# A two-layer trunk (RG-LRU, then forgetting attention) on one core: other output blocks kept on the chip, short rows' logits spread in three runs, the last squares in a tile of their own

## The chip, the core and the metric

The kernel runs on one core of a Trainium2 chip. The core has five engines, each with its own stream of instructions that it works through in order: TensorE (PE, matrix products; PEld is its loading of weights), VectorE (DVE), ScalarE (ACT), GpSimd (POOL) and SyncE (SP). SP computes nothing here: it issues transfers, as POOL does too. Transfers are carried out by 16 DMA engines. The metric is the time of one execution on the device, in microseconds (us), as the median of several runs.

## The reference

One sequence of 1024 tokens and width 1024 goes through two layers and a last norm. Everything is fp32.

```
for i in range(DEPTH):                      # DEPTH = 2
    h = rms_norm(x, norm_g[i])
    if i % 2 == 0:  x = x + lru_mixer(h, ...)   # layer 0
    else:           x = x + fox_mixer(h, ...)   # layer 1
return rms_norm(x, final_g)
```

Layer 0 (`lru_mixer`): `u = h @ w_in` (1024 to 3072) gives a branch and a gate of 1536 channels each; the branch passes a causal convolution over 4 tokens; two block-diagonal products give the gates `r` and `i`; a linear recurrence over the tokens runs with `a = exp(-8 r softplus(-a_param))`; its result times `silu(gate)` is projected back by `w_out`.

Layer 1 (`fox_mixer`), the one that the change touches most:

```
q, k, v, gate, f = split(h @ w_in)                 # 16 heads of 64
cum    = cumsum(log_sigmoid(f + b_f))              # per head
logits = q k^T / 8 + cum[query] - cum[key], causal
o      = softmax(logits) v
y      = (o * silu(gate)) @ w_out
```

## The kernel before

**Number format.** Each fp32 operand is split into a high and a low part (`hh`/`hl`, `wh`/`wl`, `yhh`/`yhl` and so on), and a product is three TensorE passes: high by high, high by low, low by high. A weight block comes by a transfer into a buffer `wf`, ScalarE casts it to `wh` (L90), and VectorE subtracts to get `wl` (L101). All matrix products are issued by the helper at L60, all plain loads of this kind by `fetch` (L56 and L57) on SP.

**Stages of a run.** Times are those of the profiled execution. Layer 0 fills the time from 0 to about 460 us. The rest is layer 1, head by head (`hd` 0 to 15). For a head there are two runs. The first multiplies the weights of queries 0 to 511 of this head with its values (`weigh(hd, 0)`, PSUM tile `O`) and makes the logits of queries 512 to 1023 (`maxima(hd, 1)`, PSUM tiles `S`, two of them). The second run does `weigh(hd, 1)` and `maxima(hd + 1, 0)`, the logits of the next head's short rows: row block i has 128(i+1) keys, so blocks 0 to 3 have 128 to 512.

**One row block in `maxima`.** TensorE makes `S`; VectorE adds the mask and finds the row maximum (L786); ScalarE takes the exponential into `p` (L791); VectorE scales the row sum and inverts it (L797, L798); ScalarE and VectorE write the high and the low half of the weights `pp` (L92, L800); SP issues a transposing transfer `pT<-pp` (L802). `weigh` reads the four blocks of `pT`. ScalarE and VectorE then collect `O` (L829, L830), and `gated` multiplies with the gate (L839) and stores the head pair's result to memory (`y1d<-yo`).

**What sets the order.** The two runs are written as strings, at L29 (`ORDER`, and `LAST` for heads 12 and on). In `run`, a digit takes one step of `weigh` (0) or `maxima` (1), and a dot takes one step of *filling* work: six matrix passes of the projections for later heads, in heads 12 to 15 of the output projection. Each step is tied behind the TensorE instruction before it. Apart from these ties a scheduler with a cost model of its own places the instructions of every engine when the program is built, so an edit in one place can change the order in others.

**Values.** After heads 3, 7 and 11 stand the values of the next four heads (`values(g)`, PSUM tiles `vps`, eight token blocks of eight products each, three passes a product). Their weights `in_wv` come in four chunks of 256 KB, two products each.

**Output.** From about 943 us on, the filling work is the output projection of the first six head pairs (`partial`, PSUM tiles `ops` of the two buffers with tag `g`): for each of 8 blocks of output channels `db` and 2 halves of tokens `c`, twelve groups of passes, plus the stored residual `x1d` (L924). Most blocks go by a round trip: POOL loads the residual (L921) into one of two buffers `xp`, VectorE adds, POOL stores it back (L926), and SP loads it once more at the end. For half 0, four blocks are *kept*: their sum stays in a tile that has become free. Blocks 3 and 2 share the tile of the gate (`sg`, named `x3`), blocks 4 to 7 the tile of one set of keys (`T0`, named `x4`). The last stage (`turned`, `finish`) adds the last two head pairs, transposes and normalizes.

**Start.** Layer 0 begins with the sum of squares of x. Half h's first seven squares are added on VectorE into one tile (`m2`); the eighth is left in a working tile (`ti`, L266) and joined by a matrix product with ones (`rsrow`). Square root and inversion (3.35 us on VectorE) give the row factor `rs`.

**Middle.** Between the layers, the sum of squares of the new x works alike (`squares`, `inv_rms`): the last block's square is a second operand of the `sscol` products for each half.

Of the kernel before, what the change touches and what calls it, by code (L numbers as in the profile page):

```python
# [16 lines left out]
AF = mybir.ActivationFunctionType  # L17
# [3 lines left out]
SEQ = 1024  # L21
HALF = 512
KT = 8
# [2 lines left out]
HD = 64  # L26
EPS = 1e-6
GROUP = 2
ORDER = "1.1..1.1..00", "1.1.1.1...0000"  # L29
LAST = "1..1..1..1..0.0", "1..1.1..1..0..0.0.0"  # L30
NEG = -1e30
PSUM = bass.MemoryType.PSUM
# [8 lines left out]
def trunk(ctx: ExitStack, tc: tile.TileContext, xt, w0, wg, wo0, pc, gn, gf, w1, wv, wf, bf, wo1, out):  # L41
    nc = tc.nc
# [16 lines left out]
    def matmul(*args, **kw):  # L59
        pe[0] = nc.tensor.matmul(*args, **kw)  # L60
        return pe[0]
# [8 lines left out]
    onesf = const.tile([P, P], F32, name="onesf")  # L70
    nc.vector.memset(onesf, 1.0)
    epst = const.tile([P, 1], F32, name="epst")
# [49 lines left out]
    def weights(src, parts=wpool, lo_eng=nc.gpsimd):  # L122

        for k in range(0, src.shape[1], 4):
            n = min(4, src.shape[1] - k)
            yield from split_weights([(src[:, k : k + n], slice(0, P))], (n, P), nc.scalar, lo_eng, parts)
# [13 lines left out]
    def drain(gen):  # L140
        for _ in gen:
            pass
# [42 lines left out]
    halves = (slice(0, HALF), slice(HALF, SEQ))  # L185

    late = ctx.enter_context(ExitStack())
    with ExitStack() as l0:
# [12 lines left out]
        def long(tag, dtype=F32, bufs=1):  # L201
            return tmp.tile([P, SEQ], dtype, tag=tag, name=tag, bufs=bufs)
# [29 lines left out]
        xs = [[xpool.tile([P, HALF], F32, name=f"x{h}{k}") for k in range(KT)] for h in range(2)]  # L232
        first = ([], [])
        early = [weights(w0[0], lo_eng=nc.vector), weights(w0[NB], lo_eng=nc.gpsimd)]
        k = 0
# [12 lines left out]
        sums = [[], []]  # L248
# [8 lines left out]

        acc = long("m2")
        sq = [z[:, cs] for z in (long("th"), long("ti")) for cs in halves]

        def square_x(h):
            to = acc[:, halves[h]]
            sums[h].append(to)
            for k in range(KT):
                z = sq[k % 4] if k else to
                nc.scalar.activation(z, xs[h][k], AF.Square)  # L266
                if k == KT - 1:
                    sums[h].append(z)
                elif k:
                    nc.vector.tensor_tensor(to, to, z, ALU.add)  # L270
                yield
# [4 lines left out]
        def norm_row(h):  # L276

            row = ps.tile([P, HALF], F32, tag="O", name="rsrow")
            for i, sq_ in enumerate(sums[h]):
                matmul(row, onesf, sq_, start=i == 0, stop=i == len(sums[h]) - 1)  # L280
            r_ = rs[:, halves[h]]
            nc.scalar.activation(r_, row, AF.Sqrt, bias=epst, scale=1.0 / SEQ)
            return nc.vector.reciprocal(r_, r_)

        for _ in zip(split_x(0), square_x(0)):
            pass
# [2 lines left out]
        state = {}  # L289
# [119 lines left out]
        for n in range(NB):  # L409
            wu = first[0] if n == 0 else list(weights(w0[n]))  # L410
            if n == 1:
                ups = both = [ps.tile([P, HALF], F32, tag="g", name="ups") for h in range(2)]
            else:
                ups = two_banks("ups")
                both = [ups.rearrange("p a b -> p (a b)")]
                ups = [ups[:, h] for h in range(2)]
            product(ups[0], 0, wu)
            if n == 0:
                gps = held[0] = two_banks("gps")
                product(gps[:, 0], 0, first[1])  # L420
                for _ in zip(split_x(1), square_x(1)):
                    pass
                done = norm_row(0)
            else:
                gates(n - 1)
                if n > 1:
                    with tc.issue_after(state[n - 1]["last"].ins):
                        outputs(n - 2)
            product(ups[1], 1, wu)
            if n == 0:  # L430
                product(gps[:, 1], 1, first[1])
                norm_row(1)
                with tc.issue_after(done.ins):
                    softplus()
            conv(n, both)
            if n % 2 and n > 1:
                fill = itertools.chain(fill, project_out((n - 3) // 2))
            take(fill, 4)
            if n > 3:
                with tc.issue_after(state[n - 1]["last"].ins):  # L440
                    take(vsquares, 4)
            if n > 1:
                wn = list(weights(w0[NB + n - 1]))
                gps = held[n - 1] = two_banks("gps")
                for h in range(2):
                    product(gps[:, h], h, wn)
            if n:
                drain(silu(state[n - 1], held.pop(n - 1)))

                with tc.issue_after(state[n]["tap"].ins):  # L450
                    recur(n - 1)
            take(fill, 4)
# [45 lines left out]
        for h, cs in enumerate(halves):  # L498
            y = [tuple(z[:, cs] for z in p) for p in ys[-2:]]
            hT[h] = [pair() for k in range(KT)]  # L500
            parts = split_x(h, 1)
            sums = []
            for d0 in range(0, KT, 4):
                pts = []
                for db in range(d0, d0 + 4):
                    if db % 2 == 0:
                        two = ps.tile([P, 2, HALF], F32, tag="S", name="ops")
                    pts.append(two[:, db % 2])
                    mm3(pts[-1], wl[db][0], y[0], True, False)
                for db, o in enumerate(pts, d0):  # L510
                    mm3(o, wl[db][1], y[1], False, True)
                    x = xs[h][db]
                    nc.vector.tensor_tensor(x, x, o, ALU.add)  # L513
                    nc.sync.dma_start(x1d[h, :, db], x)
                    next(parts)
                    squares(
                        sums,
                        x,
                        lambda: nrm.tile([P, HALF], F32, tag="sq" if db else "ss", name="sq", bufs=2),
                        wait=db == KT - 1,  # L520
                    )
            rms_row(sums, rs1[h], rms1[h])
            if h == 0:
                value_bounds()
            nc.vector.tensor_tensor(
                rv[:, :, 4 * h : 4 * h + 4],
                rms1[h].unsqueeze(1).to_broadcast([P, 4, 4]),
                scale_v.unsqueeze(2).to_broadcast([P, 4, 4]),
                ALU.mult,
            )  # L530
# [7 lines left out]
    with ExitStack() as l1:  # L538
# [190 lines left out]
        first = values(0)  # L729
# [170 lines left out]
        homes = {}  # L900

        def home(db):

            if db == 3:
                two = at.tile([P, 2, HALF], F32, tag="sg", name="x3")
                homes[3], homes[2] = two[:, 0], two[:, 1]
            elif db == 5:
                four = tu.tile([P, 4, HALF], F32, tag="T0", name="x4")
                homes.update((4 + i, four[:, i]) for i in range(4))
            return homes[db]  # L910

        def partial(todo):

            for db, c in todo:
                split_out(db)
                if c if db < 2 else not c:
                    split_out(db + 1)

                kept = c == 0 and db in (3, 5, 6, 7)
                x = home(db) if kept else rpool.tile([P, HALF], F32, tag="R", name="xp")  # L920
                nc.gpsimd.dma_start(x, x1d[c, :, db])  # L921
                pt = ps.tile([P, HALF], F32, tag="g", name="ops1")
                yield from gemm_steps(pt, zip(wo[db], [y1[c][pair] for pair in range(6)]))
                nc.vector.tensor_tensor(x, x, pt, ALU.add)  # L924
                if not kept:
                    nc.gpsimd.dma_start(x1d[c, :, db], x)  # L926
# [5 lines left out]
        def residual(c, q):  # L932

            cs = slice(q * 256, (q + 1) * 256)
            if c == q == 0:
                two = tu.tile([P, 2, HALF], F32, tag="U0", name="x0")
                homes[0], homes[1] = two[:, 0], two[:, 1]
                for d in (0, 1, 2, 4):
                    fetch(homes[d], x1d[c, :, d])
            if c == 0:  # L940
                return [homes[d][:, cs] for d in range(KT)]
            xs = [wpool.tile([P, 2, 256], F32, tag=("wl", "wh")[q], name="x1") for d in range(4)]
            for d, x in enumerate(xs):
                fetch(x, x1d[c, :, 2 * d : 2 * d + 2, cs])
            return [x[:, i] for x in xs for i in range(2)]
# [107 lines left out]
        for hd in range(HEADS):  # L1053
# [21 lines left out]
                    )  # L1075
            elif pair < 6:
                fill = chain(g_units(pair + 1), kq_units(pair + 2, ((1, (0,)),)))
            first, second = LAST if hd > 11 else ORDER
            if hd == HEADS - 1:
                first = "1..1.0.1.0.1..."  # L1080
            side = chain(pieces(hd + 1, 0, 0), pieces(hd + 1, 0, 1)) if hd else iter(())
# [105 lines left out]
```

## Time and profile before

| | us |
|---|---|
| median of 3 runs | 1081.56 (1079.12 to 1083.71) |
| profiled execution | 1079.6 |
| its span in the profile | 1077.8 |
| outside the span | 1.8 |
| TensorE busy | 1048.0 (97%) |
| VectorE busy | 782.1 (73%) |
| ScalarE busy | 621.6 (58%) |

The page of the profile lists busy time by engine and by group of instructions. A line of a group or of the timeline ends with the idle time of the engine just ahead of the instruction, and what ended it: `[5.52 <-DVE sums L797]` says that the engine stood still for 5.52 us and that VectorE's instruction of that line was the last one that it waited for. The table of windows gives busy time by stretch, the clock granted to TensorE as a share of full speed, the share of time in which the DMA engines were at work, and the rate of the transfers. Transfers on SP and POOL stand in the timeline with the time that their issue takes, not their landing. The profile names tiles without their numbers: the PSUM tile `ops1` reads `ops`, `gps1` reads `gps`, `x3` and `x4` read `x`.

### The profile page before, as it was taken

Reading aid. Unit: us, or ns where it says so; the run is one execution under the profiler, and the core shown is the slowest. Engines: PE = TensorE matmul, PEld = TensorE weight load, DVE = VectorE, ACT = ScalarE, POOL = GpSimd, SP = SyncE. Lnnn points to the kernel's source line nnn. Section 1 sums busy time; section 2 is a strip of 40 time slices with the busy share of each in tenths; the row PEclk is TensorE's granted clock in tenths of the full one; section 3 lists DMA queues with packets and bytes.
Section 4 is the critical chain, followed back from the end, with each engine's and each line's share of the span. In section 5 each row is a group of like instructions: output and inputs, shape, how many; then the busy total and the mean of one; then the engine's idle time right before and its main releaser. Section 6 shows DMA issues by size and latency. Waiting matters only on the chain. (4 is left out here: it accounts for less than half of the span.)

```text
span 1077.8 us, 14962 instructions
## 1 busy us (share of the span) xinstructions
PE 1048.0 (97%) x5100; PEld 843.7 (78%) x5100; DVE 782.1 (73%) x1444; ACT 621.6 (58%) x1082; POOL 113.2 (11%) x91
## 2 busy tenths in 40 slices
PE   9999999999999999999999999999999999997997
PEld 7788888888888887797777797767977779765776
DVE  7889657766776589947878848788488866774665
ACT  8488453655465564745757636566466655653454
POOL 1322021202220210030000000000000000011200
PEclk9999999999999999999999999999999999998999
DMA  7111211222122112535878957899578885988994
GB/s 251 60 43 50 64 59 54 64 69 64 54 70 68 49 54 69 158 94 134 157 174 192 176 135 155 179 190 191 139 153 188 174 191 131 226 210 225 224 193 157
DMA packets 218508, 142.55 MB, mean 132 GB/s; under 512 B 161792, under 2 KB 178688, under 8 KB 218432
## 3 DMA queue, kind: packets, MB, share of 16 engines
q1 hardware_dynamic: 216032, 133.74, 52.3%
q0 software_dynamic: 2400, 7.87, 2.4%
q8 instruction: 40, 0.66, 0.3%
q14 instruction: 36, 0.29, 0.1%
HBM read 63.82 MB, written 14.81 MB: 73 GB/s over the span
## 5 line engine op out<-in xcount | busy, mean ns | idle before, releaser
L60 PE MATMUL gps<-hh,wh 128*128 128x512 f32 x576 | 227.3, 395 | 0.0
L60 PE MATMUL gps<-hh,wl 128*128 128x512 f32 x576 | 226.4, 393 | 0.8 <-DVE wl L101 0.7
L60 PE MATMUL gps<-hl,wh 128*128 128x512 f32 x576 | 226.6, 393 | 0.0
L90 ACT CAST wh<-wf 128x512 fp32r<-128x512 f32 (+2 forms) x162 | 97.3, 605 | 113.5 <-PE ops L60 43.0
L791 ACT ACTIVATE p<-S,m 128x128 f32<-128x128 f32 (+7 forms) x128 | 94.7, 740 | 67.6 <-DVE m L786 37.9
L101 POOL TENSOR_TENSOR wl<-wf,wh 128x512 fp32r<-128x512 f32 (+1 forms) x50 | 91.9, 1850 | 369.9 <-ACT wh L90 358.3
L60 PEld LDWEIGHTS gps<-hl,wh 128*128 128x128 f32 x576 | 108.4, 188 | 25.0 <-issue 0.5
L60 PEld LDWEIGHTS gps<-hh,wl 128*128 128x128 f32 x576 | 108.6, 189 | 22.5 <-DVE wl L101 1.0
L60 PEld LDWEIGHTS gps<-hh,wh 128*128 128x128 f32 x576 | 108.5, 188 | 21.6
L800 DVE SCALAR_TENSOR_TENSOR pp<-p,sums,pp 128x128 f16<-128x128 f32 (+7 forms) x128 | 103.1, 814 | 19.1 <-ACT pp L92 17.9
L92 ACT ACTIVATE pp<-p,sums 128x128 f16<-128x128 f32 (+7 forms) x128 | 95.5, 770 | 31.2 <-DVE sums L798 15.6
L786 DVE CUSTOM_DVE_ANT_0 S<-S,mask 128x128 f32<-128x128 f32 (+7 forms) x128 | 97.2, 760 | 16.9 <-PE S L60 15.6
L60 PE MATMUL S<-T,U 96*128 96x512 f32 (+7 forms) x384 | 94.3, 355 | 8.1 <-ACT p L791 8.0
L101 DVE TENSOR_TENSOR wl<-wf,wh 128x512 fp32r<-128x512 f32 x112 | 74.4, 668 | 25.8 <-ACT wh L90 25.6
L60 PEld LDWEIGHTS S<-T,U 128*128 128x128 f32 (+1 forms) x384 | 67.9, 190 | 26.2 <-ACT p L791 14.3
L389 DVE TENSOR_TENSOR x<-x,ops 128x512 f32<-128x512 f32 x80 | 54.1, 683 | 41.5 <-PE ops L60 41.4
L60 PE MATMUL ups<-hh,wh 128*128 128x512 f32 x192 | 75.6, 395 | 1.2 <-ACT hh L92 1.2
L60 PE MATMUL ups<-hl,wh 128*128 128x512 f32 x192 | 76.6, 399 | 0.2
L60 PE MATMUL ops<-yh,wl 128*128 128x512 f32 x192 | 75.7, 394 | 0.9 <-DVE wl L101 0.9
L60 PE MATMUL ops<-yh,wh 128*128 128x512 f32 x192 | 75.8, 396 | 0.5 <-DVE x L513 0.5
L60 PE MATMUL ups<-hh,wl 128*128 128x512 f32 x192 | 75.8, 395 | 0.0
L60 PE MATMUL O<-pT,v 128*128 128x512 f16 (+3 forms) x396 | 71.3, 322 | 3.8 <-DMA pT<-pp 3.6
(188 smaller groups left out, 1985.8 us busy)
## 6 DMA issues: line engine op xcount, KB each, us to landing
wf<-in_w SPq DMA_DIRECT2D x106, 256.0 KB
wf<-in_wo SPq DMA_DIRECT2D x64, 128.0 KB
T<-qkh SPq DMA_DIRECT2D x64, 128.0 KB
U<-qkh SPq DMA_DIRECT2D x64, 128.0 KB
x<-in_xt SPq DMA_DIRECT2D x16, 256.0 KB
wvf<-in_wv SPq DMA_DIRECT2D x32, 128.0 KB
x1d<-x SPq DMA_DIRECT2D x16, 256.0 KB
wf<-in_wv SPq DMA_DIRECT2D x16, 256.0 KB
```

The costliest lines, as they stand in the source:

```text
L60: pe[0] = nc.tensor.matmul(*args, **kw)
L90: nc.scalar.copy(hi, src)
L92: nc.scalar.activation(hi, src, AF.Copy, scale=scale)
L101: return eng.tensor_tensor(lo, src, f32(hi), ALU.subtract)
L389: nc.vector.tensor_tensor(x, x, pt, ALU.add)
L786: nc.vector.tensor_tensor_reduce(S[:, :n], S[:, :n], mask[:, SEQ - n :], -1.0, -NEG, ALU.add, ALU.min, accum_out=m)
L791: seen[0] = nc.scalar.activation(p, S[:, :n], AF.Exp, bias=m, scale=-1.0, accum_out=sums[:, i : i + 1])
L800: nc.vector.scalar_tensor_tensor(both[:, :, 1], p, r, both[:, :, 0], ALU.mult, ALU.subtract)
```

## The change

1. **Start of layer 0.** The last square of each half goes into a tile of its own (`sg`), where before it lay in `ti`, which later squares reuse. The square root of each half is tied behind the last square issued so far, and the small work of `softplus` behind the first convolution.
2. **Middle.** For half 1 the last block's square is added on VectorE like the others, so the `sscol` products of that half have one operand and not two (four products fewer).
3. **Kept blocks.** Half 0 of blocks 4, 5, 6 and 7 is kept; before it was 3, 5, 6 and 7. The gate's tile holds blocks 4 and 3, the key tile blocks 2, 5, 6 and 7. So block 3 goes by the round trip and block 4 stays. The loads at the end fetch blocks 0 to 3 where before they fetched 0, 1, 2 and 4.
4. **Three runs.** The second run of heads 2, 6 and 10 has the string `1.1..1.1..0000` for `1.1.1.1...0000`: a second step of filling work stands ahead of the third short row block, and one fewer ahead of `weigh`.

```diff
-ORDER = "1.1..1.1..00", "1.1.1.1...0000"
+ORDER = "1.1..1.1..00", ("1.1.1.1...0000", "1.1..1.1..0000")
...
+        sq_ = long("sg")
+        squared = [None]
...
-                z = sq[k % 4] if k else to
-                nc.scalar.activation(z, xs[h][k], AF.Square)
+                z = sq_[:, halves[h]] if k == KT - 1 else sq[k % 4] if k else to
+                squared[0] = nc.scalar.activation(z, xs[h][k], AF.Square)
...
-            nc.scalar.activation(r_, row, AF.Sqrt, bias=epst, scale=1.0 / SEQ)
-            return nc.vector.reciprocal(r_, r_)
+            with tc.issue_after(squared[0].ins):
+                nc.scalar.activation(r_, row, AF.Sqrt, bias=epst, scale=1.0 / SEQ)
+            nc.vector.reciprocal(r_, r_)
...
-                with tc.issue_after(done.ins):
+            conv(n, both)
+            if n == 0:
+                with tc.issue_after(state[0]["tap"].ins):
                     softplus()
-            conv(n, both)
...
-                        wait=db == KT - 1,
+                        wait=h == 0 and db == KT - 1,
...
-            if db == 3:
+            if db == 4:
                 two = at.tile([P, 2, HALF], F32, tag="sg", name="x3")
-                homes[3], homes[2] = two[:, 0], two[:, 1]
+                homes[4], homes[3] = two[:, 0], two[:, 1]
             elif db == 5:
                 four = tu.tile([P, 4, HALF], F32, tag="T0", name="x4")
-                homes.update((4 + i, four[:, i]) for i in range(4))
+                homes.update(zip((2, 5, 6, 7), (four[:, i] for i in range(4))))
...
-                kept = c == 0 and db in (3, 5, 6, 7)
+                kept = c == 0 and db > 3
...
-                for d in (0, 1, 2, 4):
+                for d in range(4):
                     fetch(homes[d], x1d[c, :, d])
...
-            first, second = LAST if hd > 11 else ORDER
+            first, second = LAST if hd > 11 else (ORDER[0], ORDER[1][hd % 4 == 2])
```

**VectorE where block 3 of half 0 is added.** Names: `x_9163` is the kept tile of block 3 (half 0), `sg_7883` the gate's tile, `ops_9165` the products of block 3. Line numbers after the change are five higher. Before:

```order
L830 SCALAR_TENSOR_TENSOR yo<-O,unit_v,yo 64x512
L101 TENSOR_TENSOR wl<-wf,wh 128x256
L839 TENSOR_TENSOR yo<-yo,sg_7883 128x512
L797 TENSOR_SCALAR sums<-sums 128x1
L798 RECIPROCAL sums<-sums 128x1
L786 ISA S,m<-S,mask 128x768
L786 ISA m 128x1
L800 SCALAR_TENSOR_TENSOR pp<-p,sums,pp 128x5x128
L924 TENSOR_TENSOR x_9163<-x_9163,ops_9165 128x512
L797 TENSOR_SCALAR sums<-sums 128x1
```

After; here `xp` with `ops_9163` is block 3 of half 0:

```order
L835 SCALAR_TENSOR_TENSOR yo<-O,unit_v,yo 64x512
L101 TENSOR_TENSOR wl<-wf,wh 128x256
L929 TENSOR_TENSOR xp<-xp,ops_9163 128x512
L844 TENSOR_TENSOR yo<-yo,sg_7881 128x512
L802 TENSOR_SCALAR sums<-sums 128x1
L803 RECIPROCAL sums<-sums 128x1
L791 ISA S,m<-S,mask 128x768
L791 ISA m 128x1
L805 SCALAR_TENSOR_TENSOR pp<-p,sums,pp 128x5x128
L802 TENSOR_SCALAR sums<-sums 128x1
```

The addition of block 3 stands ahead of the last reading of the gate's tile, where before it stood six rows behind it. The addition of block 4, half 0, into the gate's tile stands later, behind `pp` of the 896-key block.

**SP around the values of head 3.** `wf_5453` and `wf_5459` are the third and fourth chunk of the values' weights. Before:

```order
L57 DMA U0_3679<-qkl_3724 64x512
L57 DMA wf_5381<-in_w1 128x512
L57 DMA wf_5453<-in_wv 128x512
L57 DMA wf_5459<-in_wv 128x512
L802 DMA_TRANSPOSE pT_5167<-pp_5247 128x14x128
L802 DMA_TRANSPOSE pT_5167<-pp_5268 128x16x128
```

After, the fourth chunk is `wf_5457`; it has gone from this place to the one shown here, 15 rows further on, behind the store of head 3's second half (`y1d`):

```order
L807 DMA_TRANSPOSE pT_5314<-pp_5401 128x8x128
L57 DMA T1_3675<-qkh_3679 64x512
L57 DMA T1_3675<-qkl_3680 64x512
L57 DMA y1d_3666<-yo_5142 128x512
L57 DMA wf_5457<-in_wv 128x512
L57 DMA wf_5727<-in_w1 128x512
```

The same holds at heads 7 and 11. In each of the three places ScalarE's cast of this chunk stands directly ahead of the first collection of values, and VectorE's `wl` behind `gated`.

**TensorE in the values of head 3.** `vps_5465` (before) and `vps_5463` (after) are the first token block; `wh_5461` (before) and `wh_5459` (after) come from the fourth chunk. Before, the first pass with the fourth chunk is the 31st of the values:

```order
L60 MATMUL vps_5465<-wh_5455,hh_3385 128x256
L60 MATMUL vps_5465<-wh_5455,hl_3386 128x256
L60 MATMUL vps_5465<-wl_5456,hh_3385 128x256
L60 MATMUL vps_5465<-wh_5461,hh_3387 128x256
L60 MATMUL vps_5465<-wh_5461,hl_3388 128x256
L60 MATMUL vps_5465<-wl_5462,hh_3387 128x256
```

After, it is the 73rd; all four PSUM tiles of the first token blocks have had their first six products by then:

```order
L60 MATMUL vps_5556<-wh_5453,hh_3386 128x256
L60 MATMUL vps_5556<-wh_5453,hl_3387 128x256
L60 MATMUL vps_5556<-wl_5454,hh_3386 128x256
L60 MATMUL vps_5463<-wh_5459,hh_3388 128x256
L60 MATMUL vps_5463<-wh_5459,hl_3389 128x256
L60 MATMUL vps_5476<-wh_5459,hh_3388 128x256
L60 MATMUL vps_5476<-wh_5459,hl_3389 128x256
```

The fourth chunk is used 42 passes later. On SP, the load of block 2's residual for the last stage (`x4<-x1d`, 256 KB) now stands ahead of the last two transposes of head 14, where before a load of block 4 stood behind those of head 15's first half. The number of instructions is the same on each engine but for four `sscol` products fewer on TensorE and one addition more on VectorE.

More of the change, by code (lines that the diff above doesn't have):

```diff
@@ L278, in norm_row @@
             row = ps.tile([P, HALF], F32, tag="O", name="rsrow")
-            for i, sq_ in enumerate(sums[h]):
-                matmul(row, onesf, sq_, start=i == 0, stop=i == len(sums[h]) - 1)
+            for i, z in enumerate(sums[h]):
+                matmul(row, onesf, z, start=i == 0, stop=i == len(sums[h]) - 1)
             r_ = rs[:, halves[h]]
-            nc.scalar.activation(r_, row, AF.Sqrt, bias=epst, scale=1.0 / SEQ)
-            return nc.vector.reciprocal(r_, r_)
+            with tc.issue_after(squared[0].ins):
+                nc.scalar.activation(r_, row, AF.Sqrt, bias=epst, scale=1.0 / SEQ)
+            nc.vector.reciprocal(r_, r_)
         for _ in zip(split_x(0), square_x(0)):
@@ L422, in trunk @@
                     pass
-                done = norm_row(0)
+                norm_row(0)
             else:
```

## The prediction

> **What bounds the kernel now.** I read the page first, then TensorE's waits, then the timeline of each engine around the longest of them, and the windows for the granted clock. The busy line of the page:
>
> ```profile
> PE 1048.0 (97%) x5100; PEld 843.7 (78%) x5100; DVE 782.1 (73%) x1444; ACT 621.6 (58%) x1082; POOL 113.2 (11%) x91
> ```
>
> TensorE is the bound: of the span of 1077.8 us it stands still for 29.8 us, and some of that is the end of the program. An edit can gain only from those gaps, from passes left out, or from a clock that was lowered. TensorE's waits, longest sums first (us in total, times, longest):
>
> ```profile
> PE S L60 <- ACT p L791: 8.0, 9, 2.1
> PE ops L60 <- DVE sums L797: 5.5, 1, 5.5
> PE O L60 <- DMA pT<-pp: 3.6, 5, 1.4
> ```
>
> The middle row is one single wait. In TensorE's timeline (start, duration, idle time ahead) it is:
>
> ```profile
> 984.27 1.08 PE L60 MATMUL S<-T,U 128*128 128x512 f32 x4 [0.31 <-ACT p L791]
> 990.87 0.80 PE L60 MATMUL ops<-yhh,wh 128*128 128x512 f32 x1 [5.52 <-DVE sums L797]
> 996.16 1.13 PE L60 MATMUL S<-T,U 128*128 128x512 f32 x4
> 997.12 0.40 PE L60 MATMUL ops<-yhh,wh 128*128 128x512 f32 x1
> 999.92 0.93 PE L60 MATMUL O<-pT,v 128*128 128x512 f16 x4
> ```
>
> The releaser named had long been done; the real one stands in VectorE's and POOL's timelines, and in the list of transfers (the last figure is the landing):
>
> ```profile
> 984.40 0.69 DVE L839 TENSOR_TENSOR yo<-yo,sg 128x512 f32<-128x512 f32 x1
> 986.31 0.89 DVE L800 SCALAR_TENSOR_TENSOR pp<-p,sums,pp 128x640 f16<-128x640 f32 x1
> 990.13 0.69 DVE L924 TENSOR_TENSOR x<-x,ops 128x512 f32<-128x512 f32 x1 [2.93 <-DMA x<-x1d]
> 985.38 0.54 POOL L921 DMA_DIRECT2D x<-x1d  x1 [3.53 <-DVE sums L798]
> x<-x1d POOLq DMA_DIRECT2D x1, 256.0 KB, 4.7
> ```
>
> POOL can load block 3's residual into the gate's tile only after the last reading of that tile (L839, 984.40 plus 0.69). The load is issued at 985.38 and lands 4.7 us later. VectorE, in order, waits for it; both `ops` tiles are full; TensorE waits for VectorE. The clock then pays as well:
>
> ```profile
> 868.00:872.00 4.00, 1.89 (x9) 1.23 (x8) 3.08 (x8) 1.57 (x4) 0.00 (x0) 1.00 0.93 245
> 988.00:992.00 4.00, 1.13 (x3) 0.94 (x4) 1.87 (x5) 0.24 (x1) 0.00 (x0) 0.67 0.74 141
> 992.00:996.00 4.00, 4.00 (x11) 3.13 (x10) 2.73 (x8) 2.90 (x4) 0.79 (x2) 0.50 0.59 182
> 50.00:400.00 350.00, 350.00 (x1516) 284.67 (x1515) 251.77 (x263) 199.81 (x281) 74.49 (x38) 1.00 0.20 59
> ```
>
> The columns after the busy times are granted clock, DMA share and GB/s. Behind the 5.52 us wait the clock is 0.67 and 0.50; behind a wait of about 2 us, at 868 to 872, it stays 1.00. The twelve passes from 990.87 took 5.29 us (to 996.16), the next twelve 2.80 us (997.12 to 999.92): 2.49 us lost to the clock.
>
> **The change part by part.**
>
> *Start.* The last row above has no TensorE gap from 50 to 400 us. The change moves half 1's `rsrow` behind seventeen more passes, some 4 us at 2.80/12 = 0.23 us a pass. The products in between hide it; if that cover is gone, TensorE waits for a PSUM tile that VectorE scales with the row factor. I take 0; bounds 0 and +4.
>
> *Middle.* Four products fewer are eight passes:
>
> ```profile
> 463.45 1.62 PE L60 MATMUL sscol<-onesf,sq 128*128 128x1 f32 x14
> ```
>
> 1.62/14 = 0.116 us a pass, so -0.9 us. The added VectorE addition runs beside value products; if not hidden it costs the 0.68 us of such an addition (L839 above). I take -0.9; bounds -0.9 and 0.
>
> *Three runs.* TensorE at the third short row block (128x384) and at `weigh` of heads 6 and 10 (and head 2), and the last two pairs of transposes on SP, the second field being the time of their issue:
>
> ```profile
> 586.70 0.62 PE L60 MATMUL S<-T,U 128*128 128x384 f32 x2 [0.76 <-ACT p L791]
> 711.76 0.50 PE L60 MATMUL S<-T,U 128*128 128x256 f32 x2 [0.60 <-ACT p L791]
> 715.28 0.62 PE L60 MATMUL S<-T,U 128*128 128x384 f32 x2 [1.62 <-ACT p L791]
> 841.85 0.62 PE L60 MATMUL S<-T,U 128*128 128x384 f32 x2 [1.07 <-ACT p L791]
> 714.70 5.11 SPq L802 DMA_TRANSPOSE pT<-pp  x2
> 721.84 1.47 PE L60 MATMUL O<-pT,v 128*128 128x512 f16 x6
> 841.27 6.07 SPq L802 DMA_TRANSPOSE pT<-pp  x2
> 848.82 1.47 PE L60 MATMUL O<-pT,v 128*128 128x512 f16 x6 [0.29 <-DMA pT<-pp]
> ```
>
> One more filling step (6 passes, 1.4 us) covers the gaps at the 128x384 blocks: 0.76 + 1.40 + 1.07 = 3.2 us. But filling is only moved: the step is missing ahead of `weigh`, which then arrives that much earlier and needs the transposes of long rows that ScalarE and VectorE finished before. In head 10 `weigh` already waits; it starts 1.48 us after the issue has ended (847.34). By the same 1.48 us, head 6's transposes land at 719.81 + 1.48 = 721.3, only 0.55 us ahead of `weigh`. So head 10 gains nothing, head 6 at most 0.55, head 2 at most its 0.76. Late next is the transpose. I take half of 1.3, -0.6; bounds -3.2 and +1.
>
> *Kept blocks.* Block 3's addition no longer waits for a tile: its `xp` is one of the loads that POOL issued before, and the addition stands ahead of L839. The 5.52 us and the 2.49 us go: -8.0. POOL then loads block 4's tile at about 986, and by the same 4.7 us it lands at about 991; its addition stands behind `pp` of the 896-key block, so VectorE does not come to it much sooner. What is late next is head 14's last transposes:
>
> ```profile
> 999.65 10.86 SPq L802 DMA_TRANSPOSE pT<-pp  x2
> 1014.47 1.04 PE L60 MATMUL O<-pT,v 128*128 128x512 f16 x4 [0.80 <-DMA pT<-pp]
> ```
>
> SP needs 10.86 us to issue this pair, where head 6's took 5.11: the DMA engines are behind. `weigh` already waits 0.80 us for it, and would now arrive 8 us earlier. The pair is ready earlier too, since its logits stand behind the removed stall, but the transfers ahead of it are the same, with one load of 256 KB more on SP (block 2) and one store more on POOL (block 3's round trip). The DMA share gives room of 0.26 x 4 + 0.41 x 4 = 2.7 us in the windows 988 to 996. If the DMA engines set the pace, no more than 2.7 us of the 8.0 stay; if the pair simply moves with its logits, all 8.0 do. I take the middle, -5.0 after rounding down for the two added transfers; bounds -8.0 and -2.
>
> [...]
>
> *The fourth chunk of the values' weights*, which the diff doesn't name. Start of the values, the 73rd pass of head 3's, and the place in SP's queue that the chunk now has (that of `wf<-in_w` behind `y1d`):
>
> ```profile
> 623.30 0.36 PE L60 MATMUL vps<-wh,hh 128*128 128x256 f32 x1
> 631.89 0.28 PE L60 MATMUL vps<-wh,hh 128*128 128x256 f32 x1
> 750.15 0.37 PE L60 MATMUL vps<-wh,hh 128*128 128x256 f32 x1
> 879.05 0.37 PE L60 MATMUL vps<-wh,hh 128*128 128x256 f32 x1
> 620.52 2.97 PE L60 MATMUL O<-pT,v 128*128 128x512 f16 x16 [1.38 <-DMA pT<-pp]
> 630.14 0.94 SPq L57 DMA_DIRECT2D wf<-in_w  x2
> 740.10 5.69 SPq L802 DMA_TRANSPOSE pT<-pp  x2
> 756.86 1.20 SPq L57 DMA_DIRECT2D wf<-in_w  x2
> 886.51 0.96 SPq L57 DMA_DIRECT2D wf<-in_w  x2
> 738.46 0.59 SPq L57 DMA_DIRECT2D wf<-in_w  x1
> 741.50 0.62 ACT L90 CAST wh<-wf 128x512 fp32r<-128x512 f32 x1 [1.35 <-DMA wf<-in_w]
> ```
>
> The pass that needs it comes 631.89 - 623.30 = 8.6 us after the start: at 631.9, 758.7 and 887.6. A load of this size takes 3.0 us from issue to cast (738.46 to 741.50) up to the 4.7 us of the POOL load; I take 4.0, and 0.6 for the cast. With the slots as they are, the chunk is ready at 634.7, 761.5 and 891.1: stalls of 2.8, 2.8 and 3.5 us, 9.1 in all (11.2 with 4.7 us). But SP reaches that slot earlier, because 256 KB less stand ahead of the two transposes (5.69 us of issue at 740.10, against some 1.2 us for one small one): I take 2 us. Then the stalls are 0.8, 0.8 and 1.5 us, 3.1 in all. Head 3's `weigh`, which waits 1.38 us behind these transfers, may gain up to 1.4 us, but the values then start earlier by as much and wait longer for the chunk, so I count nothing there. I take +3.0; bounds -1.4 (chunk in time, head 3's wait gone) and +11.2.
>
> **Sum.** -0.9 - 0.6 - 5.0 + 3.0 = -3.5 us. Against the profiled execution's 1079.6 us that is 1076.1. The median of the runs stands 2.0 us above the profiled one, so the forecast is 1078. About 0.5%, 5.4 us, is what a measurement of this kernel can tell from no change, so this is within it.
>
> **Rivals.**
>
> *A. The whole gain stays.* The transposes of head 14 move with their logits and the fourth chunk is in time: -0.9 - 0.6 - 8.0 - 1.4 = -10.9, so 1070.7. For it: the DMA engines have room in 988 to 996, and SP is relieved at heads 3, 7 and 11. Against it: the 10.86 us of issue and three places that all have to go well. 25%.
>
> *B. The values stall in full, and the clock drops: slower.* SP's slot does not move, and all three loads take 4.7 us: stalls of 3.5, 3.5 and 4.2 us, +11.2. With the other terms the sum is +4.7, 1086. If the clock falls behind each stall as it did behind the 5.52 us, three times 2.49 us come on top: 1094. [...] For it: the queue slots of the rows. Against it: a wait of 2 us left the clock at 1.00. [...] The trace has 5.52 us with a lowered clock and about 2 us without, nothing between. 15%.
>
> *C. The wait only moves to head 14's `weigh`.* The DMA engines are the limit, 2 us of the 8.0 stay, the rest as in the sum: -0.5, so 1081. For it: the wait of 0.80 us that is already there. Against it: the room of 2.7 us. 10%.
>
> **Chances.** The forecast has 50%, with 1073 to 1083 as its own range. Faster by over 0.5% (below 1076.2): A and the lower sixth of the forecast, 0.33. Slower by over 0.5% (above 1087.0): most of B, and a little for the start's bound, 0.14. Within: 0.53. The range reaches to A and to B without the clock: 1070.5 to 1088.
>
> **What the next profile would show.** TensorE's wait of 5.5 us for `ops` is gone and the clock is 1.00 from 985 to 1000, or the kept-blocks step is wrong. A new longer wait of `O` for `pT` in head 14 would show how much came back: 3 us by the forecast, none by A, 6 by C. New waits of `vps` for `wh` at heads 3, 7 and 11 of 0.8 to 1.5 us bear out the fourth chunk's step; over 3 us with a clock below 1.00 is B. The waits of `S` for `p` in heads 2, 6 and 10 become smaller and those of `O` for `pT` there larger. What would make me wrong beyond this is a change of the scheduler's order in a place that I took as neutral, above all in layer 0, where a new TensorE gap would show.

## The result and the profile after

The changed kernel takes 1097.18 us (median of 4 runs, 1094.01 to 1098.82) against 1082.05 us before (4 runs, 1079.12 to 1083.71). The ratio is 1.0139, 95% interval 1.0107 to 1.0171: slower by 1.4%. The forecast was 1078 us with a range up to 1088.

The span of the profiled execution is 1097.0 us, where before it was 1077.8 us: 19.2 us longer (it is the slowest of its four runs, so a little more than the medians' 15.1 us). First the page's busy line, then TensorE's longest waits (us in total, times, longest):

```profile
PE 1055.6 (96%) x5092; PEld 848.1 (77%) x5092; DVE 785.1 (72%) x1445; ACT 621.4 (57%) x1082; POOL 106.4 (10%) x91
```

```profile
PE vps L60 <- ACT wh L90: 12.8, 3, 5.6
PE O L60 <- DMA pT<-pp: 9.7, 6, 3.7
PE S L60 <- ACT p L796: 4.8, 6, 1.9
```

TensorE has eight passes fewer and yet is busy 7.6 us longer: some passes ran at a lower clock. The 5.5 us wait for `ops` is gone, and the waits for `p` fell from 8.0 to 4.8 us. In their place stand three waits of the values for a weight cast, which were not there before, and 6.1 us more of waits for transposes. TensorE's timeline at these places:

```profile
594.66 4.67 PE L60 MATMUL O<-pT,v 128*128 128x512 f16 x16 [1.88 <-DMA pT<-pp]
625.13 0.36 PE L60 MATMUL vps<-wh,hh 128*128 128x256 f32 x1
637.35 0.58 PE L60 MATMUL vps<-wh,hh 128*128 128x256 f32 x1 [3.44 <-ACT wh L90]
654.21 0.31 PE L60 MATMUL S<-T,U 128*128 128x320 f32 x1
769.82 0.58 PE L60 MATMUL vps<-wh,hh 128*128 128x256 f32 x1 [3.76 <-ACT wh L90]
907.29 0.58 PE L60 MATMUL vps<-wh,hh 128*128 128x256 f32 x1 [5.60 <-ACT wh L90]
1032.16 1.89 PE L60 MATMUL O<-pT,v 128*128 128x512 f16 x4 [3.68 <-DMA pT<-pp]
```

SP's and ScalarE's side of the first two waits of the values: the two transposes of long rows, the store and the fourth chunk in SP's queue, and ScalarE's cast of that chunk, which stood idle for 10 us until the load landed:

```profile
614.03 5.99 SPq L807 DMA_TRANSPOSE pT<-pp  x2
630.93 0.54 SPq L57 DMA_DIRECT2D y1d<-yo  x1
631.51 0.43 SPq L57 DMA_DIRECT2D wf<-in_wv  x1
636.68 0.62 ACT L90 CAST wh<-wf 128x512 fp32r<-128x512 f32 x1 [10.10 <-DMA wf<-in_wv]
746.80 5.64 SPq L807 DMA_TRANSPOSE pT<-pp  x2
764.71 0.43 SPq L57 DMA_DIRECT2D wf<-in_wv  x1
769.14 0.62 ACT L90 CAST wh<-wf 128x512 fp32r<-128x512 f32 x1 [10.13 <-DMA wf<-in_wv]
```

The windows around these waits and around head 14's show the granted clock (the column after the busy times):

```profile
632.00:636.00 4.00, 1.92 (x17) 1.72 (x15) 0.00 (x0) 0.00 (x0) 0.00 (x0) 1.00 0.90 242
636.00:640.00 4.00, 2.65 (x12) 2.65 (x13) 0.69 (x1) 0.62 (x1) 0.00 (x0) 0.52 0.84 193
640.00:644.00 4.00, 4.00 (x25) 4.00 (x24) 2.18 (x7) 2.58 (x8) 0.00 (x0) 0.63 0.39 104
644.00:648.00 4.00, 4.00 (x36) 4.00 (x35) 1.05 (x3) 0.77 (x3) 0.00 (x0) 1.00 0.00 0
769.27:772.68 3.41, 2.87 (x13) 2.87 (x14) 0.69 (x1) 0.49 (x1) 0.00 (x0) 0.50 0.94 240
772.68:776.10 3.42, 3.15 (x27) 2.98 (x26) 2.38 (x8) 2.44 (x8) 0.00 (x0) 1.00 0.34 102
906.00:910.00 4.00, 2.71 (x12) 2.71 (x13) 0.69 (x1) 0.62 (x1) 0.00 (x0) 0.50 0.67 151
1032.00:1036.00 4.00, 3.84 (x10) 2.48 (x11) 0.75 (x3) 1.20 (x3) 0.00 (x0) 0.57 0.75 208
```

The lag of the changed kernel behind the one before, read at the same instruction in both timelines, gives the account. Each row is how far the lag grew in that stretch.

| stretch | before, at its end | after, at its end | lag grew by |
|---|---|---|---|
| layer 0 (to the first value product) | 460.59 | 462.02 | +1.4 |
| middle (to the logits at 505.88) | 505.88 | 506.43 | -0.9 |
| to the end of head 2 | 596.32 | 599.14 | +2.3 |
| to the values of head 3 | 623.30 | 625.13 | -1.0 |
| values after head 3 | 646.10 | 654.21 | +6.3 |
| to the values of head 7 | 750.15 | 757.26 | -1.0 |
| values after head 7 | 772.95 | 785.96 | +5.9 |
| to the values of head 11 | 879.05 | 892.87 | +0.8 |
| values after head 11 | 901.86 | 924.02 | +8.3 |
| output and end | 1077.8 | 1097.0 | -2.9 |

The values account for 20.5 us, more than the whole loss: 13.1 us of waits (the three above and one of 0.27 us) and 7.4 us of passes at a lower clock.

### The profile page after: what moved, and what is told of

The parts are those of the page before. It is cut to its first block, busy times and chain, and to the rows that moved or that the text cites. A ratio compares the mean times of both kernels' runs of the same rounds, so it can differ in the third digit from the quotient of the medians.

```text
span 1097.0 us, 14944 instructions
## 1 busy us (share of the span) xinstructions
PE 1055.6 (96%) x5092; PEld 848.1 (77%) x5092; DVE 785.1 (72%) x1445; ACT 621.4 (57%) x1082; POOL 106.4 (10%) x91
## 5 line engine op out<-in xcount | busy, mean ns | idle before, releaser
L60 PEld LDWEIGHTS gps<-hh,wl 128*128 128x128 f32 x576 | 108.6, 189 | 22.7 <-DVE wl L101 1.0
L101 POOL TENSOR_TENSOR wl<-wf,wh 128x512 fp32r<-128x512 f32 (+1 forms) x50 | 85.1, 1712 | 378.2 <-ACT wh L90 314.7
L60 PE MATMUL vps<-wh,hh 128*128 128x256 f32 (+1 forms) x256 | 75.8, 299 | 13.1 <-ACT wh L90 12.8
L60 PE MATMUL O<-pT,v 128*128 128x512 f16 (+3 forms) x396 | 73.8, 330 | 9.7 <-DMA pT<-pp 9.7
```

The lines of the kernel that those rows point to most:

```text
L101: return eng.tensor_tensor(lo, src, f32(hi), ALU.subtract)
```

## The experiments

**One part undone, one part alone.** Run e1_no_order puts the string of the changed kernel back, with the line that picks it:

```diff
-ORDER = "1.1..1.1..00", ("1.1.1.1...0000", "1.1..1.1..0000")
+ORDER = "1.1..1.1..00", "1.1.1.1...0000"
...
-            first, second = LAST if hd > 11 else (ORDER[0], ORDER[1][hd % 4 == 2])
+            first, second = LAST if hd > 11 else ORDER
```

> The changed kernel with the run string of heads 2, 6 and 10 put back; start, middle and kept blocks stay changed. Theory Q (queue): the string alone sent the fourth chunk of the values' weights behind the store y1d, and the three waits of the values for it (3.44, 3.76 and 5.60 us) and the lowered clock behind them are the loss. Then those waits are gone, and what is left is the start (+1.4), the middle (-0.9) and the kept blocks (-2.9): 1079.6 us, ratio to the kernel before 0.998. Rival S (start or kept blocks moved it): the three waits stay and the time is 1095 us or more.

Measured: 1079.16 us, ratio 0.9995 (0.9972 to 1.0019). The waits of the values are gone. TensorE's waits, and the one that is left in head 14:

```profile
PE O L60 <- DMA pT<-pp: 7.5, 8, 4.1
PE S L60 <- ACT p L796: 6.9, 6, 1.6
1011.16 1.89 PE L60 MATMUL O<-pT,v 128*128 128x512 f16 x4 [4.08 <-DMA pT<-pp]
```

So start, middle and kept blocks together change next to nothing. Run e2_order_alone makes the same edit, the other way round, in the kernel before:

```diff
-ORDER = "1.1..1.1..00", "1.1.1.1...0000"
+ORDER = "1.1..1.1..00", ("1.1.1.1...0000", "1.1..1.1..0000")
...
-            first, second = LAST if hd > 11 else ORDER
+            first, second = LAST if hd > 11 else (ORDER[0], ORDER[1][hd % 4 == 2])
```

> The kernel before with only the run string of heads 2, 6 and 10 changed. Theory Q: the waits of the values for the fourth chunk appear (13 us with some 7.7 us of clock), and head 2's longer wait of O for pT: +21.6 us, 1103.6 us, ratio 1.020. Rival S: the waits are not there and the time is within 3 us of the kernel before.

Measured: 1101.79 us, ratio 1.0205 (1.0166 to 1.0245).

```profile
PE vps L60 <- ACT wh L90: 12.0, 3, 4.5
PE O L60 <- DMA pT<-pp: 8.5, 6, 2.7
PE ops L60 <- DVE x L924: 5.8, 1, 5.8
```

The string alone makes the loss. Theory Q holds against rival S: the edit concerns heads 2, 6 and 10, and most of what it costs (18 of the 22.9 us by which this profile is longer) lies one head later.

**Is it the place in SP's queue?** Run e3_chunk_by_pool leaves the string changed and issues the fourth chunk from POOL:

```diff
+                loads_by[0] = nc.gpsimd if k == 6 and not ex else nc.sync
                 parts += split_weights(src, (2, 256 + ex), nc.scalar, nc.gpsimd if ex else nc.vector)
+                loads_by[0] = nc.sync
```

> The changed kernel, its run string included, but the fourth chunk of the values' weights is issued by POOL, which has nothing to do in that stretch, in place of SP. Theory Q: what makes TensorE wait is the place in SP's queue, so the load is issued as soon as its buffer is free, the waits of the values vanish with their clock loss: 1097.2 - 20.5 = 1076.7 us, ratio 0.995. Rival D (the DMA engines): the same 256 KB run again beside the transposes of long rows, so the waits move to O for pT at heads 3, 7 and 11, and no more than half is won: 1086 us or more. The waits of O for pT in heads 2, 6 and 10 (1.6 to 1.9 us) stay by both.

Measured: 1088.17 us, ratio 1.008 (1.0055 to 1.0105). That is in the range of rival D (1086 or more) and far from Q's 1076.7: the loss against the kernel before falls from 15 to 9 us. The values wait no more, and the chunk is again first used by the 31st pass. But a longer wait of `S` for `p` has come, in TensorE's timeline and in ScalarE's, with POOL's issue and the window behind the first of them. The last two lines show another difference that the edit brought: the sixteen products of `weigh` of head 3, which stood ahead of the values, now stand behind their first 14 passes (heads 7 and 11 alike).

```profile
610.72 0.70 POOL L57 DMA_DIRECT2D wf<-in_wv  x1 [140.40 <-DVE wl L101]
616.10 0.62 ACT L90 CAST wh<-wf 128x512 fp32r<-128x512 f32 x1 [3.25 <-DMA wf<-in_w]
617.24 0.80 PE L60 MATMUL S<-T,U 128*128 128x512 f32 x2 [2.06 <-ACT p L798]
616.00:620.00 4.00, 2.76 (x8) 2.19 (x9) 2.70 (x8) 1.57 (x4) 0.00 (x0) 0.72 1.18 256
747.63 1.22 PE L60 MATMUL S<-T,U 128*128 128x512 f32 x2 [2.41 <-ACT p L798]
879.40 0.74 PE L60 MATMUL S<-T,U 128*128 128x512 f32 x2 [2.75 <-ACT p L798]
623.53 0.28 PE L60 MATMUL vps<-wh,hh 128*128 128x256 f32 x1
625.20 2.99 PE L60 MATMUL O<-pT,v 128*128 128x512 f16 x16
```

POOL issues the chunk as soon as its buffer is free, at 610.72 (VectorE's `wl` ended POOL's idle time). At head 3 ScalarE then waits 3.25 us for the load of the next projection's weights (1.31 us at this cast in the kernel before), and the cast starts 7.04 us after the weight cast ahead of it (609.06 to 616.10), where it took 5.11 us (608.02 to 613.13). The exponentials of the next row blocks stand behind it, and TensorE waits for these: 2.06 us, where the kernel before has no wait (614.27). At head 7 this wait is 2.41 us, against 0.17 there (742.64). At head 11 the kernel before had it too, 2.11 us at 871.54, and there it only grew, to 2.75. So the place in SP's queue was what made the values wait, and rival D is right in so far as other waits have grown. That this shows at `S` for `p` and not at `O` for `pT` proves little, since `weigh` comes later here. Around heads 3, 7 and 11 this profile still falls 8.2 us behind the kernel before; how much of that is the longer wait for the load and how much the new order of TensorE is left open. At head 14, `O` waits 5.71 us.

**The kept blocks alone.** Run e4_kept_alone is the kernel before with the edits of `home`, `partial` and `residual`:

```diff
-            if db == 3:
+            if db == 4:
...
-                kept = c == 0 and db in (3, 5, 6, 7)
+                kept = c == 0 and db > 3
...
-                for d in (0, 1, 2, 4):
+                for d in range(4):
```

> The kernel before with only the kept blocks changed. Theory K: the wait of 5.5 us for ops and its clock loss (8.0 us) go, and 5.1 us of it come back as a wait of O for pT in head 14 and the clock behind that, as in the changed kernel: -2.9 us, 1079.2 us, ratio 0.997. Rival F (full gain): in the changed kernel head 14 came 20 us later and met other transfers; here the wait does not return: -7.5 us or more, 1074.5 us.

Measured: 1078.47 us, ratio 0.9977 (0.9957 to 0.9998). The wait for `ops` is gone, and one place later stands this:

```profile
1010.84 1.89 PE L60 MATMUL O<-pT,v 128*128 128x512 f16 x4 [5.08 <-DMA pT<-pp]
```

TensorE is 8.1 us ahead of the kernel before at the products that stood at 999.92, 3.6 us ahead behind this wait, and 1.0 us at the end; 0.5 us of it were there ahead of the place, at 976.57. Theory K holds: most of the 8 us come back.

**What makes head 14's wait.** In SP's queue three residual loads of 256 KB stand directly ahead of the pair of transposes, where in the kernel before there were two. Run e6_kept_and_middle has the kept blocks and the middle; run e7_residual_late also ties the residual loads behind later transposes:

```diff
-                for d in range(4):
-                    fetch(homes[d], x1d[c, :, d])
+                for d, lag in enumerate((9, 9, 7, 6)):
+                    with tc.issue_after(turns[-lag].ins):
+                        fetch(homes[d], x1d[c, :, d])
```

Run e8_both_late besides spreads POOL's loads for the kept blocks 6 and 7:

```diff
-        homes = {}
+        homes, stores = {}, []
...
-                nc.gpsimd.dma_start(x, x1d[c, :, db])
+                with tc.issue_after(stores[-2].ins) if kept and db > 5 else ExitStack():
+                    nc.gpsimd.dma_start(x, x1d[c, :, db])
...
-                    nc.gpsimd.dma_start(x1d[c, :, db], x)
+                    stores.append(nc.gpsimd.dma_start(x1d[c, :, db], x))
```

> The kernel before with the kept blocks and the middle changed. The parts add up: kept blocks -1 us (measured alone: ratio 0.998), middle -0.9 us (eight passes): -2 us, ratio 0.998, and O of head 14 waits 4 to 5 us for pT with a lowered clock behind it. If the middle is hidden work after all, ratio 0.999.

> As e6_kept_and_middle, with SP's four residual loads (256 KB each) for blocks 0 to 3 behind head 14's last transposes, where three of them stood directly ahead. Theory L (loads ahead): they are what makes the wait of O for pT in head 14; 768 KB at the 250 to 310 GB/s of these windows are 2.5 to 3.1 us, so the wait falls from 5 to 2 us and the clock stays up (1.6 us): -4.5 us against e6, ratio 0.994. Rival T (transposes themselves): the pair of 896 and 1024 keys with POOL's three loads fills the DMA engines anyway, the wait stays 4 us or more, ratio 0.998.

> As e7_residual_late, with POOL's loads for kept blocks 6 and 7 each behind one more store, where all three stood together at head 14's last transposes. Theory L: 512 KB less beside the pair, some 2 us: the wait of O for pT falls below 1 us, -1.5 us against e7, ratio 0.9925. Rival: the additions of blocks 6 and 7 wait for these loads and TensorE for the PSUM tiles, +2 us or more against e7.

Measured: e6 1077.50 us, ratio 0.9974 (0.9958 to 0.9989); e7 1076.14 us, ratio 0.9979 (0.9957 to 1.0002); e8 1076.13 us, ratio 0.9958 (0.9937 to 0.9978). SP's queue and the wait in e6, then in e7:

```profile
994.88 1.33 SPq L57 DMA_DIRECT2D x<-x1d  x3
996.30 13.04 SPq L802 DMA_TRANSPOSE pT<-pp  x2
1011.48 1.89 PE L60 MATMUL O<-pT,v 128*128 128x512 f16 x4 [6.14 <-DMA pT<-pp]
```

```profile
993.32 8.33 SPq L802 DMA_TRANSPOSE pT<-pp  x2
1005.42 1.02 PE L60 MATMUL O<-pT,v 128*128 128x512 f16 x4 [1.09 <-DMA pT<-pp]
1007.86 0.50 PE L60 MATMUL ops<-yhh,wh 128*128 128x512 f32 x1 [1.42 <-DVE sums L797]
```

Theory L holds in the profiles: without the three loads the wait falls from 6.14 to 1.09 us and the pair's issue from 13.04 to 8.33 us. The profiled span of e7 is 1071.4 us, that of e6 1076.6 us. But the profile of e7 is that of the fastest of its twelve runs, which lie between 1073.2 and 1083.6 us. The medians differ by only 1.4 us, the ratio is no lower than that of e6, and the 0.994 that L foretold lies outside its interval: how much of the 5 us stays in a typical run is left open. In e8 head 14's `weigh` starts at 1007.97 without a wait in the profile. Its median is that of e7, and the intervals of the two ratios overlap, so the further gain of 1.5 us that L foretold is not shown. e8 beats both kernels, the one before by 0.4%.

**The start alone.** Run e5_start_alone has the `sg` tile, the two ties and the moved `softplus`, and nothing else of the change (two places of its edit):

```diff
-                z = sq[k % 4] if k else to
+                z = sq_[:, halves[h]] if k == KT - 1 else sq[k % 4] if k else to
...
-                with tc.issue_after(done.ins):
-                    softplus()
-            conv(n, both)
+            conv(n, both)
+            if n == 0:
+                with tc.issue_after(state[0]["tap"].ins):
+                    softplus()
```

> The kernel before with only the start of layer 0 changed. Theory: in the changed kernel and in run e1_no_order TensorE is 1.4 to 2.1 us behind at 460 us, with a new wait of gate for wgl (0.8 us at 101 us); the start alone makes this: +1.5 us, ratio 1.0014. Rival: this is the time at which the inputs arrive, which changes from run to run: within 0.3 us.

Measured: 1081.13 us, ratio 1.0011 (0.9992 to 1.0030). In its profile TensorE is 1.75 us behind at 460 us, with the same new wait as in the changed kernel:

```profile
101.79 0.74 PE L60 MATMUL gate<-xch,wgl 128*128 128x512 f32 x2 [0.81 <-DVE wgl L101]
```

The interval of the times contains both theories, but the profiles decide against the rival. Counted from the first `rsrow` product at about 19 us, which leaves out the arrival of the inputs, the way to the first value product at 460 us is 1.6 to 1.7 us longer in all four profiles with the new start (the changed kernel, e1, e3, e5), and within 0.05 us the same in the five others.

## Why the prediction was wrong

*The step that failed* is the fourth chunk of the values' weights, as a term that was mis-sized: +3.0 us stood in the sum, 20.5 us were measured. These are 17.5 of the 22.7 us by which the profile lies above the forecast's sum. The mechanism was the right one, and it is rival B, which had 15% and 1094 us. Three numbers of the step were off.

- "But SP reaches that slot earlier ... I take 2 us." It did not. Relative to the start of the values the slot was 6.8, 6.7 and 7.5 us behind before (630.14, 756.86, 886.51) and 6.4, 7.5 and 8.0 us after (631.51, 764.71, and 900.92 at head 11). The pair of transposes that should have become quicker took 5.64 us at head 7, against 5.69 before, and 5.68 at head 11, against 5.89; only head 3's became clearly shorter, 5.99 against 7.88. Between the pair and the slot SP also issues the transposes of the next head's short rows, and waits for VectorE to write their weights (1.2 us for `pp` in each of the stretches 618 to 632 and 752 to 765).
- "I take 4.0" for the load. From issue to cast it took 5.2, 4.4 and 5.7 us, two of the three above the upper end of 4.7 taken from one load. With the real slots and loads and 0.7 us for the cast, against the 8.6 us of cover, the step gives 3.6, 4.0 and 5.8 us: the measured waits to 0.3 us.
- The clock. I put it in rival B alone. Behind the three waits it fell to 0.50, for 6.83, 3.41 and 6.83 us, and cost 7.4 us in all. B's price of three times 2.49 us was right to 0.1 in the sum by luck: the three cost 2.8, 1.9 and 2.7 us. The clock also fell behind waits of 1.88 us (head 2, to 0.50) and 2.06 us (e3, 0.72 from 616 to 620), shorter than any stall that I had priced with it (3.5 us). The wait of 2.11 us that I had read as harmless was split over two steps of the clock, as the last section shows.

The range ended at 1088 because B counted only without the clock there; a stall that I had priced above 3 us at its upper end belonged into the range with its clock.

*Three runs.* Forecast -0.6 us at heads 2, 6 and 10, since the gap comes back as a wait for the transposes. That exchange happened: the gap at 715.28 fell from 1.62 to 0.21 us, and `O` of head 6, without a wait before, waits 1.60 us. But the size was missed, beyond the bound of +1. From the end of the first to the end of the second `weigh` of heads 2, 6 and 10 the changed kernel falls behind the kernel before by 3.7 us in all, e2 with the string alone by 2.3, and e1 without the string by 1.7. Only e3 against e1 (1.3 and 1.7) looks like the forecast. What was not in the term is again the clock: behind head 2's wait of 1.88 us in the changed kernel the sixteen products took 4.67 us, in e3 2.99 us, and behind head 10's wait of 2.75 us in e2 they took 4.67 us too.

*Kept blocks.* Forecast -5.0, with -8.0 and -2 as bounds; measured -2.9 in the changed kernel. In the other profiles less stays from 976.57 on: e1 wins 1.7 us, e4 0.6, and e6 loses 0.5. The wait and the clock loss went as said, the gain came back at head 14's `weigh` as said, and more of it than I took: 3.68 to 6.14 us. The second cost, a lowered clock behind the new wait (0.57), was not in the term. The room of 2.7 us in the DMA engines comes near the -2.9 of the changed kernel, but is more than the others kept.

*Middle.* Forecast -0.9 us, measured -0.9 in the account and in the profile of e6 (0.01 ahead at 460.59, 0.88 ahead at 505.88).

*Start.* Forecast 0 with +4 as the far bound; +1.4 to +2.1 us at 460 us in the profiles, or 1.6 to 1.7 us when counted from 19 us on. Part of the loss is not where I looked (a PSUM tile that is scaled with the row factor) but at 101 and 103 us: two waits, together 1.0 us, for low parts that VectorE makes. Where the rest lies was not found.

## What to carry to other kernels

Where a scheduler places the instructions, an edit's price lies wherever the order changed; compare the two orders whole, and work out for each transfer that moved when it is needed and when it can be there, with the slowest like transfer of the profile and without a relief that no row shows. A wait as long as those behind which the profiles show a lowered clock (here from 1.88 us, though not behind each one of about 2 us) is to be priced with it. And what a removed stall gives can come back at the next transfer: here the 5.52 us for `ops` went, and 3.68 to 6.14 us came back at head 14's `weigh`. Look at what stands directly ahead of that transfer in the queue, and move that too: without the three loads the pair's issue took 8.33 us, not 13.04.

## What the runs showed of the hardware that was not expected

The lowered clock came with shorter waits than the 5.52 us one, and not from one length on. In the changed kernel a wait of 1.88 us, which ended at 594.66, was followed by a clock of 0.50, while waits of 1.89 us in the same kernel and of 2.11 us in the kernel before left it at 1.00:

```profile
885.39 0.73 PE L60 MATMUL S<-T,U 128*128 128x512 f32 x2 [1.89 <-ACT p L796]
871.54 0.74 PE L60 MATMUL S<-T,U 128*128 128x512 f32 x2 [2.11 <-ACT p L791]
```

Read in finer windows, the clock of the kernel before and of the changed kernel is always 1.00 or 0.50. Between 20 and 1065 us a lowered stretch lasts 3.41 or 6.83 us. The one of the kernel before starts at 989.39; the five of the changed kernel start at 595.19, 636.15, 769.27, 905.80 and 1032.10, whole multiples of 3.41 us apart. So each of these two profiles can be cut into steps of 3.41 us, here for the waits of 1.88 and 1.89 us (the changed kernel) and of 2.11 us (the kernel before); the first figure behind the comma is TensorE's busy time:

```profile
591.78:595.19 3.41, 1.53 (x8) 0.77 (x7) 2.91 (x9) 3.22 (x8) 0.00 (x0) 1.00 0.88 190
595.19:598.60 3.41, 3.41 (x10) 1.19 (x9) 1.04 (x2) 0.25 (x1) 0.00 (x0) 0.50 0.51 106
881.91:885.32 3.41, 1.58 (x8) 0.98 (x6) 2.68 (x7) 1.07 (x4) 0.00 (x0) 1.00 0.94 232
885.32:888.73 3.41, 3.34 (x15) 2.76 (x16) 2.81 (x9) 1.69 (x5) 0.00 (x0) 1.00 1.19 226
```

```profile
866.51:869.92 3.41, 2.92 (x14) 2.10 (x12) 3.31 (x7) 0.58 (x3) 0.00 (x0) 1.00 0.90 218
869.92:873.34 3.42, 1.80 (x8) 1.48 (x9) 2.56 (x9) 1.57 (x4) 0.00 (x0) 1.00 1.09 264
873.34:876.75 3.41, 3.41 (x17) 2.46 (x16) 2.06 (x6) 2.29 (x6) 0.00 (x0) 1.00 0.94 229
```

The wait of 1.88 us lies whole in one step; that of 1.89 us has 1.83 us in one, and that of 2.11 us is split, 0.49 and 1.62 us. In these two profiles, over the same time, all six steps at full clock in which TensorE stood still for 1.88 us or more (1.88, 2.23, 3.21 and three times 3.41 us) were followed by a lowered one, and none of those with 1.83 us or less. In e8 less was enough: a wait of 2.06 us, which ended at 985.23, was followed by a clock of 0.86 from 984 to 988 and of 0.71 from 988 to 992. A lowered stretch of 0.50 with these means starts at about 986.9, and 1.7 to 1.8 us of the wait lie in the 3.41 us ahead of that (an estimate from these windows). So what parts the waits of about 2 us in these profiles seems to be the idle time within one step, not the length of the wait, and no sharp limit is shown. This is read from the profiles; no run was made to try it.
